# A hybrid SSD and S5 layer: the input projection in two blocks of tokens, each weight tile used twice

## The chip, the cores and the metric

One core of a Trainium2 chip. The metric is the device time in microseconds of one execution. The engines are TensorE (PE, with its weight loads PEld), VectorE (DVE), ScalarE (ACT), GpSimd (POOL) and SyncE (SP), whose queue issues most transfers.

## The reference, cut to what matters

One layer over 1024 prompt tokens and 32 sample tokens, which share the weights:

```
xn = rmsnorm(x, pre_mix_norm_w)
proj = xn @ w_in
z, xbc, dt_raw, u_s5 = split(proj)          # 512, 1024, 8 and 512 columns
y_ssd = ssd_mixer(z, xbc, dt_raw, ...)      # conv of 4 taps + SiLU on xbc, chunked scan, * silu(z), rmsnorm
y_s5  = s5_mixer(u_s5, ...)                 # complex diagonal recurrence, gelu, per-group GLU
h = x + rmsnorm(concat([y_ssd, y_s5]) @ w_out, post_mix_norm_w)
up = causal_dwconv(rmsnorm(h, pre_ffn_norm_w) @ w_up)       # 3 taps
y = h + rmsnorm((gelu(gate) * val) @ w_down, post_ffn_norm_w)
```

## The kernel before

Everything is feature-major: features on partitions, the 1056 tokens along the free axis. Tokens are cut into three chunks of 512, 272 and 272 (`CHUNKS`, L22); chunk 0 is block 0, chunks 1 and 2 are block 1. All products are exact to fp32: weights and activations are split into a high and a low part in fp32r, and `mm3` (L439) makes three products (high by high, high by low, low by high) for each 128 rows of the contraction. With eight such pieces a tile of 128 outputs and one chunk takes 24 products.

**Weights.** `w_load` (L415) brings one tile of 128x1024 from memory (`raw`, two buffers, a transfer of 512 KB on SP), `w_split` (L423) makes the high part on ScalarE (`wh`, a copy by the helper at L253) and the low part on DVE (`wl = raw - wh`, L431); both have two buffers. The sequence of tiles is a list, `order` (L409): sixteen input tiles, then the second half of the output projection's rows for block 0 (`outh`, from S5), its first half (`outs[0]`, from SSD), the same for block 1, and the tiles of the feed-forward network.

**Input projection.** Tiles 0 to 3 give `u` (for S5), 4 to 11 `xBC` (for SSD), 12 to 15 `z` (its gate). Each tile is loaded and split once and used for the three chunks in turn (`gemm_in`, L569); only the last two z tiles are taken as 14 for chunk 0, 15 for chunk 0, then both for the rest (`gemm_z`, L585), so that block 0's z ("zA") is there early. An accumulator (`pm`, from a ring in PSUM) is freed by its evacuation: `evac_xbc` (L483) takes one DVE step (L489) for chunk 0, and then the convolution of block 0 (three DVE steps at L495 on `xo`, with a scaled copy and a SiLU on ScalarE), for the other chunks L500 and L502; `evac_z` (L525) takes two DVE steps (L530, L532) with a tanh on ScalarE in the accumulator between them, and stores z in memory (L533).

**Side work.** Generators are stepped between the products: the S5 preparations and its eight runs (each ends with `y5s`, L923, and a store), `conv_b` (L508; block 1's convolution, eight tiles with three steps at L518 on `xob` and one at L520), `s5mix` (L1238; it reads the results of S5 back in 32 transfers and makes the high and low parts of the mixed features 4 to 7), the SSD scan of block 0 (`frontsA`, `backsA`, `gatesA`), and later, in the feed-forward part, the same of block 1 (`frontsB`, `backsB`, `gatesB`). A generator that yields a name waits for it: `conv_b` begins with `yield par["cvat"]`, which is "run7", the last run of S5. The framework's scheduler then orders the instructions of each engine by data and by priority, so that the order in the program is only a wish.

Of the kernel before, what the change touches and what calls it, by code (L numbers as in the profile page):

```python
# [21 lines left out]
CHUNKS = [(0, WA), (WA, HB), (WA + HB, T - WA - HB)]  # L22
# [25 lines left out]
           cvat='run7', tcat=1, late_at=2, nsq=1, fg=(), fp=((1, 3), (1, 3), (3,)), fch=(0, (0, 1), 2), pfin=0, q0=0, q1=0, q2=0, nb=0,   # L48
# [128 lines left out]
def body(tc, xT, wt, wdt, vec, cst, dtp, hist4, hist3, h0ssd, s5p, s5bc, s5d, glu, glub,  # L177
# [5 lines left out]
    par = dict(PAR)  # L183
# [4 lines left out]
    done = set()  # L188

    def mm(out, lhsT, rhs, start=True, stop=True, **kw):  # L190
        n = rhs.free_size() if hasattr(rhs, "free_size") else int(np.prod(rhs.shape[1:]))
        m = int(np.prod(lhsT.shape[1:]))
        if lhsT.dtype == F32R:
            clk[0] += max(n / 2.36, 107 if m > 64 else 62) * 1e-3
        else:
            clk[0] += max(n * 1.69, 214 if m > 64 else 120) * 1e-3
        PE.matmul(out, lhsT, rhs, start=start, stop=stop, **kw)  # L197
# [34 lines left out]
    def side(name, gen, prio=0, ch=0):  # L232
        sides.append(Side(gen, name, prio, ch))

    def run_main(gen):
        for _ in gen:
            for s in list(sides):
                if s.ready():
                    s.step()
# [12 lines left out]
    def act(out, in_, func, scale=1.0, bias=0.0):  # L252
        S.activation(out, in_, func, bias=bias, scale=scale)  # L253
# [22 lines left out]
    def pmt():  # L276
        pch[1] += 1
        ch = pch[0][pch[1] % len(pch[0])]
        return ms.tile([128, 512], F32, name="pm", tag=f"ms{ch}", bufs=par["msb"][ch])
# [123 lines left out]
    WT = {}  # L403
    ob = par["ob_at"]
    outh = [("out", q) for q in range(4)]
    outs = [[("out", 4 + q, b) for q in range(4)] for b in range(2)]
    ups = [("up", j) for j in range(2 * FF)]
    outh2 = [o + (1,) for o in outh[par["nb"]:]]
    order = [("in", j) for j in range(16)] + outh + outs[0] + outh2 + [u + (0,) for u in ups[:ob]]  # L409
    order += outs[1] + [u + (0,) for u in ups[ob:]] + [u + (1,) for u in ups]  # L410
    seq = [{"in": WIN, "out": WOUT, "up": WUP}[o[0]] + o[1] for o in order]
    pos = {o: i for i, o in enumerate(order)}
# [2 lines left out]
    def w_load(n):  # L415
        while st["load"] <= min(n, len(seq) - 1):
            i = st["load"]
            r = ring.tile([128, 1024], F32, name="raw", tag="raw", bufs=2)
            D.dma_start(r, wt[seq[i]])
            WT[i] = [r]  # L420
            st["load"] += 1

    def w_split(n):  # L423
        while st["split"] <= min(n, len(seq) - 1):
            i = st["split"]
            w_load(i)
            r = WT[i][0]
            hi = ring.tile([128, 1024], F32R, name="wh", tag="wh", bufs=2)
            lo = ring.tile([128, 1024], F32R, name="wl", tag="wl", bufs=2)
            act(hi, r, AF.Copy)  # L430
            V.tensor_tensor(lo, r, hi.bitcast(F32), sub)  # L431
            WT[i] = [hi, lo]
            st["split"] += 1

    def xsl(x, c):
        o = CHUNKS[c][0] - BLK[c > 0][0]
        return [t[:, :, o:o + CHUNKS[c][1]] for t in x[c > 0]]

    def mm3(ps, w, x, ks, first, last):  # L439
        for k in ks:  # L440
            wh, wl = w[0][:, k * 128:k * 128 + 128], w[1][:, k * 128:k * 128 + 128]
            xh, xl = x[0][:, k, :], x[1][:, k, :]
            mm(ps, wh, xh, start=(k == first), stop=False)
            mm(ps, wh, xl, start=False, stop=False)
            mm(ps, wl, xh, start=False, stop=(k == last))
# [7 lines left out]
    X = {}  # L453
# [29 lines left out]
    def evac_xbc(j, c, ps):  # L483
        t0, w = CHUNKS[c]
        eb = XB[1][:, j, :]
        if c == 0:
            e = XB[0][:, j, :3 + WA]
            G.memset(e[:, 0:3], 0.0)
            V.tensor_tensor(e[:, 3:], ps[:, :w], rbc[:, t0:t0 + w], mult)  # L489
            G.tensor_copy(eb[:, 0:3], e[:, WA:])  # L490
            G.tensor_copy(eb[:, 3 + TP - WA:6 + TP - WA], hist4_t[:, j, :])
            o = tl("xo", [128, WA], "xo")
            act(o, e[:, 0:WA], AF.Identity, scale=vc("cw", 4 * j), bias=vc("cb", j))
            for i in range(1, 4):
                V.scalar_tensor_tensor(o, e[:, i:i + WA], vc("cw", 4 * j + i), o, mult, add)  # L495
            act(XB[0][:, j, :WA], o, AF.Silu)
            return
        o = 3 + t0 - WA
        wp = min(w, TP - t0)
        V.tensor_tensor(eb[:, o:o + wp], ps[:, :wp], rbc[:, t0:t0 + wp], mult)  # L500
        if w > wp:
            V.tensor_tensor(eb[:, EB - TS:], ps[:, wp:w], rbc[:, TP:], mult)  # L502
            G.tensor_copy(o4[:, j, 0, :], eb[:, TP - WA:TP - WA + 3])
            G.tensor_copy(o4[:, j, 1, :], eb[:, EB - 3:])
            if j == 7:
                D.dma_start(o_conv, o4)

    def conv_b():  # L508
        yield par["cvat"]
        n = EB - 3  # L510
        cwh = con.tile([128, 40], F32, name="cwh")
        V.tensor_scalar(cwh, vc("cw", 0, 40), 0.5, None, mult)
        for j in range(8):
            e = XB[1][:, j, :]
            o, th = tl(("bc", "PQ")[j % 2], [128, n], "xob"), e[:, 0:n]
            act(o, e[:, 0:n], AF.Identity, scale=cwh[:, 4 * j:4 * j + 1], bias=cwh[:, 32 + j:33 + j])
            for i in range(1, 4):
                V.scalar_tensor_tensor(o, e[:, i:i + n], cwh[:, 4 * j + i:4 * j + i + 1], o, mult, add)  # L518
            act(th, o, AF.Tanh)
            V.scalar_tensor_tensor(e[:, 0:n], th, 1.0, o, add, mult)  # L520
            yield par["cvb"]
# [3 lines left out]
    def evac_z(j, c, ps):  # L525
        t0, w = CHUNKS[c]
        zc[0] += 1
        ps = ps[:, :w]
        zt = tl(("xo", "xe")[zc[0] % 2], [128, 512], "zst")[:, :w]
        V.scalar_tensor_tensor(zt, ps, 0.5, rbc[:, t0:t0 + w], mult, mult)  # L530
        act(ps, zt, AF.Tanh)
        V.scalar_tensor_tensor(zt, ps, 1.0, zt, add, mult)  # L532
        D.dma_start(z_dram[:, j, t0:t0 + w], zt)  # L533
# [32 lines left out]
        w_split(2)  # L566
        yield

    def gemm_in(j0, j1, evac):  # L569
        for j in range(j0, j1):  # L570
            w_split(j)
            for c in range(3):
                t0, w = CHUNKS[c]
                ps = pmt()
                mm3(ps[:, :w], WT[j], xsl(X, c), range(4), 0, 7)
                if c == 0:
                    w_load(j + 2)
                yield
                mm3(ps[:, :w], WT[j], xsl(X, c), range(4, 8), 0, 7)
                evac(j, c, ps)  # L580
                if c == 1:
                    w_split(j + 1)
                yield

    def gemm_z():  # L585
        yield from gemm_in(12, 14, lambda j, c, ps: evac_z(j - 12, c, ps))
        w_split(14)
        for j, c in ((14, 0), (15, 0), (14, 1), (14, 2), (15, 1), (15, 2)):
            t0, w = CHUNKS[c]
            ps = pmt()  # L590
            mm3(ps[:, :w], WT[j], xsl(X, c), range(4), 0, 7)
            if c == 0:
                w_load(j + 2)
            yield
            mm3(ps[:, :w], WT[j], xsl(X, c), range(4, 8), 0, 7)
            evac_z(j - 12, c, ps)
            if j == 15 and c == 0:
                done.add("zA")
            if (j, c) == (14, 0):
                w_split(15)  # L600
            if (j, c) == (14, 2):
                w_split(16)
            yield
        done.add("zdone")

    small = {}

# [425 lines left out]
    pch[0] = par["pch0"]  # L1033
    run_main(gemm_in(3, 4, evac_u))
    run_main(dt_gemm())
    run_main(gemm_in(4, 12, lambda j, c, ps: evac_xbc(j - 4, c, ps)))
    done.add("xbc")
    state = {}
    SC, MIX = {}, {}
# [172 lines left out]
    def fronts(b):  # L1212
        if b:
            yield "convb"
        else:
            for n in ("xbc", "dt", "prep7", "run6"):
                yield n
        for c in SSDC[b]:
            n = 1 if b else 2
            if c - n >= SSDC[b][0]:  # L1220
                yield f"back{c - n}"
            yield from ssd_front(c)
            done.add(f"front{c}")
# [168 lines left out]
            act(rbc[:, t0:t0 + w], norm_r(list(accs.values()), w, scrt("U0", ("W1", "W0")[b]), None, f"p{c}"), AF.Copy)  # L1392
        yield 0

    side("convb", conv_b())
    side("s5mix", s5mix(), par["pg"])
    side("frontsA", fronts(0), par["pf"], par["cf"])
    side("backsA", backs(0), par["pb"], par["cb"])
    side("gatesA", gates_a(), par["pgt"], par["cg"])
    run_main(gemm_z())  # L1400
    finish("s5mix")
    pch[0] = par["pch1"]
    run_main(gemm_outh())
# [215 lines left out]
    def fin_block(b):  # L1619
# [7 lines left out]
        for c in BLKC[b]:  # L1627
            yield from fin_mm(c)
            side(f"fin{c}", fin_out(c), par["pfin"], par["fch"][c])

    side("frontsB", fronts(1), 0, par["cf2"])
    side("backsB", backs(1), 0, par["cb2"])
    side("gatesB", gates(1), 0, par["cg2"])
# [28 lines left out]
```

## Time and profile before

| what | us |
|---|---|
| three runs: median (lowest to highest) | 1337.19 (1330.95 to 1337.25) |
| the profiled execution's own time | 1333.72 |
| its span | 1331.9 |
| PE, PEld, DVE busy in it | 1246.3, 1119.5, 1006.5 |
| ACT, POOL busy in it | 576.4, 403.6 |

The input projection lies between some 30 and 345 us of the span, the first block's output projection begins at 345.6 (second half of its rows) and 395 us, and from there to the end stands the feed-forward network, with the second block's SSD scan beside its first part. The times of rows are microseconds from the span's start. The granted clock of TensorE is given as a share of its full 2.4 GHz.

### The profile page before, as it was taken

How to read it: one execution, taken by the hardware profiler on the slowest of the kernel's cores; microseconds unless marked ns; L12 is line 12 of the kernel's file. 1: busy time of each engine (PE TensorE's matmuls, PEld its weight loads, DVE VectorE, ACT ScalarE, POOL GpSimd, SP SyncE). 2: the span in 40 equal slices, each digit the busy share in tenths (PEclk: the TensorE clock that was granted, in tenths of full speed). 3: DMA queues.
4: the chain of work that ended last, by engine and by line, in shares of the span. 5: the costliest groups of instructions: out<-in, count | busy, mean ns of one | idle time of the engine just before them, and what ended most of it. 6: DMA issues, size and time to landing. Idle time of an engine off the chain costs nothing.

```text
span 1331.9 us, 20957 instructions
## 1 busy us (share of the span) xinstructions
PE 1246.3 (94%) x7880; PEld 1119.5 (84%) x7880; DVE 1006.5 (76%) x1781; ACT 576.4 (43%) x984; POOL 403.6 (30%) x577
## 2 busy tenths in 40 slices
PE   7799889999869899999999999999899999999994
PEld 6678889888748787877897878889899999999994
DVE  8857886996764878887759986677767777777777
ACT  7335655554433545544335433335343333333343
POOL 5453545433424723421035310001511001101013
PEclk9898999999879899999999989999899999999997
DMA  7051333225214532234333333222332222222211
GB/s 229 34 154 41 98 93 98 86 77 141 76 46 135 170 119 88 72 103 129 122 122 113 96 134 95 95 95 80 111 96 95 80 96 82 93 86 87 78 56 68
DMA packets 66902, 132.15 MB, mean 99 GB/s; under 512 B 13936, under 2 KB 34800, under 8 KB 66800
## 3 DMA queue, kind: packets, MB, share of 16 engines
q1 hardware_dynamic: 66800, 130.81, 31.1%
q8 instruction: 62, 1.02, 0.3%
q14 instruction: 40, 0.33, 0.1%
HBM read 111.69 MB, written 15.81 MB: 96 GB/s over the span
## 4 chain that ended last, share of the span: by engine, by line
PE 72%; DVE 15%; ACT 3%; issue 2%; DMA 1%; POOL 1%; SPq 1%; DVEq 0%; ACTq 0%; POOLq 0%
PE pm L197 65%; PE ms L197 7%; DVE wl L431 2%; DVE o L1377 2%; DVE ftmp L1456 1%; DVE acc L1609 1%; DVE xob L518 1%; DVE xo L495 1%; DVE xl L1380 1%; ACT xh L253 1%; DMA raw<-wt 1%; DVE yr L822 1%; DMA y<-yd 0%; PE ms L201 0%; DVE fext L1439 0%
## 5 line engine op out<-in xcount | busy, mean ns | idle before, releaser
L197 PE MATMUL pm<-xh,wh 128*128 128x272 f32 (+1 forms) x1616 | 536.4, 333 | 19.8 <-ACT xh L253 8.7
L197 PE MATMUL pm<-xh,wl 128*128 128x272 f32 (+1 forms) x1616 | 534.5, 332 | 11.6 <-DVE wl L431 11.6
L197 PE MATMUL pm<-xl,wh 128*128 128x272 f32 (+1 forms) x1616 | 533.9, 330 | 0.7 <-DVE xl L763 0.7
L197 PEld LDWEIGHTS pm<-xh,wh 128*128 128x128 f32 x1616 | 312.6, 194 | 44.9 <-ACT xh L253 9.5
L197 PEld LDWEIGHTS pm<-xh,wl 128*128 128x128 f32 x1616 | 311.9, 193 | 34.3 <-DVE wl L431 12.7
L197 PEld LDWEIGHTS pm<-xl,wh 128*128 128x128 f32 x1616 | 312.3, 193 | 23.8 <-DVE xl L763 1.6
L253 ACT ACTIVATE wh<-raw 128x1024 fp32r<-128x1024 f32 x120 | 126.6, 1055 | 175.7 <-PE pm L197 125.7
L431 DVE TENSOR_TENSOR wl<-raw,wh 128x1024 fp32r<-128x1024 f32 x120 | 157.1, 1310 | 43.1 <-ACT wh L253 42.7
L197 PE MATMUL pm<-ah,dh 128*128 128x272 f32 (+1 forms) x528 | 173.1, 328 | 2.1 <-DVE fext L1439 1.3
L197 PE MATMUL pm<-ah,dl 128*128 128x272 f32 (+1 forms) x528 | 172.3, 326 | 0.0
L197 PE MATMUL pm<-al,dh 128*128 128x272 f32 (+1 forms) x528 | 172.1, 326 | 0.0
L1511 DVE TENSOR_TENSOR acc<-acc,pm 128x272 f32<-128x272 f32 (+1 forms) x235 | 121.0, 520 | 55.4 <-PE pm L197 55.0
L1456 DVE SCALAR_TENSOR_TENSOR ftmp<-fext,vec_t,ftmp 128x512 f32<-128x512 f32 (+1 forms) x176 | 138.4, 788 | 1.7 <-ACT ftmp L253 1.0
L1439 DVE TENSOR_TENSOR fext<-pm,rbc 128x512 f32<-128x512 f32 (+2 forms) x132 | 67.2, 510 | 74.3 <-PE pm L197 70.9
L1434 POOL COPY fext<-halo 128x2 f32<-128x2 f32 x88 | 38.0, 432 | 263.6 <-DVE ftmp L1456 245.5
L253 ACT ACTIVATE dh<-raw 128x1024 fp32r<-128x1024 f32 (+1 forms) x46 | 46.8, 1022 | 162.6 <-PE pm L197 135.4
L197 PEld LDWEIGHTS pm<-ah,dh 128*128 128x128 f32 x528 | 99.8, 189 | 11.1 <-DVE fext L1439 2.0
L197 PEld LDWEIGHTS pm<-ah,dl 128*128 128x128 f32 x528 | 99.7, 189 | 8.2
L197 PEld LDWEIGHTS pm<-al,dh 128*128 128x128 f32 x528 | 99.8, 189 | 7.5
L253 ACT ACTIVATE ftmp<-fext,vec_t 128x512 f32<-128x512 f32 (+1 forms) x88 | 72.1, 821 | 20.4 <-DVE fext L1441 13.2
L1489 DVE TENSOR_TENSOR dl<-raw,dh 128x1024 fp32r<-128x1024 f32 (+1 forms) x46 | 54.6, 1188 | 25.1 <-ACT dh L253 24.7
L1451 POOL COPY o<-fext 128x2 f32<-128x2 f32 x44 | 13.8, 313 | 174.8 <-DVE fext L1439 174.8
(318 smaller groups left out, 1693.3 us busy)
## 6 DMA issues: line engine op xcount, KB each, us to landing
raw<-wt SPq DMA_DIRECT2D x164, 512.0 KB, 3.3
gluw<-glu SPq DMA_DIRECT2D x8, 512.0 KB, 4.1
xst<-xT SPq DMA_DIRECT2D x16, 136.0 KB, 4.3
pbd<-pbo SPq DMA_DIRECT2D x8, 272.0 KB, 3.8
xr<-xT SPq DMA_DIRECT2D x8, 272.0 KB, 3.0
pbi<-pbd SPq DMA_DIRECT2D x8, 272.0 KB, 2.8
yT<-acc SPq DMA_DIRECT2D x8, 272.0 KB, 2.2
ud<-uext SPq DMA_DIRECT2D x4, 528.0 KB, 2.9
```

Source lines behind the costliest of these rows:

```text
L197: PE.matmul(out, lhsT, rhs, start=start, stop=stop, **kw)
L253: S.activation(out, in_, func, bias=bias, scale=scale)
L431: V.tensor_tensor(lo, r, hi.bitcast(F32), sub)
L495: V.scalar_tensor_tensor(o, e[:, i:i + WA], vc("cw", 4 * j + i), o, mult, add)
L518: V.scalar_tensor_tensor(o, e[:, i:i + n], cwh[:, 4 * j + i:4 * j + i + 1], o, mult, add)
L1377: V.scalar_tensor_tensor(h, h, vc("post_mix", k), r1, mult, mult)
L1434: G.tensor_copy(e[:, 0:2], halo[:, j, :])
L1439: V.tensor_tensor(e[:, 2 + o:2 + o + wp], ps[:, :wp], rbc[:, t0:t0 + wp], mult)
L1451: G.tensor_copy(o3[:, j, 0, :], e[:, TP - WA:TP - WA + 2])
L1456: V.scalar_tensor_tensor(t, e[:, i:i + n], vc("fw", 3 * j + i), t, mult, add)
L1489: V.tensor_tensor(l, rr, h.bitcast(F32), sub)
L1511: V.tensor_tensor(a, a, ps[:, :w], add)
```

## The change

The list of tiles gets twelve entries more: tiles 4 to 15 are in it twice. `u` is computed for all tokens as before; then tiles 4 to 15 for chunk 0 alone, then 4 to 15 for chunks 1 and 2, with each weight tile fetched and split again (offset 12 in the sequence). `gemm_z` goes. `conv_b` loses its wait for "run7" and is registered just before `frontsB`, at the start of the feed-forward network's side work, instead of ahead of `s5mix`. Line numbers behind the change are 18 lower from L606 on.

```diff
--- before.py
+++ after.py
@@ -406,7 +406,7 @@
     outs = [[("out", 4 + q, b) for q in range(4)] for b in range(2)]
     ups = [("up", j) for j in range(2 * FF)]
     outh2 = [o + (1,) for o in outh[par["nb"]:]]
-    order = [("in", j) for j in range(16)] + outh + outs[0] + outh2 + [u + (0,) for u in ups[:ob]]
+    order = [("in", j) for j in range(16)] + [("in", j, 1) for j in range(4, 16)] + outh + outs[0] + outh2 + [u + (0,) for u in ups[:ob]]
     order += outs[1] + [u + (0,) for u in ups[ob:]] + [u + (1,) for u in ups]
     seq = [{"in": WIN, "out": WOUT, "up": WUP}[o[0]] + o[1] for o in order]
     pos = {o: i for i, o in enumerate(order)}
@@ -506,7 +506,6 @@
                 D.dma_start(o_conv, o4)
 
     def conv_b():
-        yield par["cvat"]
         n = EB - 3
         cwh = con.tile([128, 40], F32, name="cwh")
         V.tensor_scalar(cwh, vc("cw", 0, 40), 0.5, None, mult)
@@ -566,42 +565,25 @@
         w_split(2)
         yield
 
-    def gemm_in(j0, j1, evac):
+    def gemm_in(j0, j1, evac, chunks=range(3), off=0):
         for j in range(j0, j1):
-            w_split(j)
-            for c in range(3):
+            i = j + off
+            w_split(i)
+            for c in chunks:
                 t0, w = CHUNKS[c]
                 ps = pmt()
-                mm3(ps[:, :w], WT[j], xsl(X, c), range(4), 0, 7)
-                if c == 0:
-                    w_load(j + 2)
+                mm3(ps[:, :w], WT[i], xsl(X, c), range(4), 0, 7)
+                if c == chunks[0]:
+                    w_load(i + 2)
                 yield
-                mm3(ps[:, :w], WT[j], xsl(X, c), range(4, 8), 0, 7)
+                mm3(ps[:, :w], WT[i], xsl(X, c), range(4, 8), 0, 7)
                 evac(j, c, ps)
-                if c == 1:
-                    w_split(j + 1)
+                if c == chunks[len(chunks) // 2]:
+                    w_split(i + 1)
                 yield
 
-    def gemm_z():
-        yield from gemm_in(12, 14, lambda j, c, ps: evac_z(j - 12, c, ps))
-        w_split(14)
-        for j, c in ((14, 0), (15, 0), (14, 1), (14, 2), (15, 1), (15, 2)):
-            t0, w = CHUNKS[c]
-            ps = pmt()
-            mm3(ps[:, :w], WT[j], xsl(X, c), range(4), 0, 7)
-            if c == 0:
-                w_load(j + 2)
-            yield
-            mm3(ps[:, :w], WT[j], xsl(X, c), range(4, 8), 0, 7)
-            evac_z(j - 12, c, ps)
-            if j == 15 and c == 0:
-                done.add("zA")
-            if (j, c) == (14, 0):
-                w_split(15)
-            if (j, c) == (14, 2):
-                w_split(16)
-            yield
-        done.add("zdone")
+    def evac_xz(j, c, ps):
+        (evac_xbc if j < 12 else evac_z)(j - 4 if j < 12 else j - 12, c, ps)
 
     small = {}
 
@@ -1033,7 +1015,7 @@
     pch[0] = par["pch0"]
     run_main(gemm_in(3, 4, evac_u))
     run_main(dt_gemm())
-    run_main(gemm_in(4, 12, lambda j, c, ps: evac_xbc(j - 4, c, ps)))
+    run_main(gemm_in(4, 12, evac_xz, (0,)))
     done.add("xbc")
     state = {}
     SC, MIX = {}, {}
@@ -1392,12 +1374,14 @@
             act(rbc[:, t0:t0 + w], norm_r(list(accs.values()), w, scrt("U0", ("W1", "W0")[b]), None, f"p{c}"), AF.Copy)
         yield 0
 
-    side("convb", conv_b())
     side("s5mix", s5mix(), par["pg"])
     side("frontsA", fronts(0), par["pf"], par["cf"])
     side("backsA", backs(0), par["pb"], par["cb"])
     side("gatesA", gates_a(), par["pgt"], par["cg"])
-    run_main(gemm_z())
+    run_main(gemm_in(12, 16, evac_xz, (0,)))
+    done.add("zA")
+    run_main(gemm_in(4, 16, evac_xz, (1, 2), 12))
+    done.add("zdone")
     finish("s5mix")
     pch[0] = par["pch1"]
     run_main(gemm_outh())
@@ -1628,6 +1612,7 @@
             yield from fin_mm(c)
             side(f"fin{c}", fin_out(c), par["pfin"], par["fch"][c])
 
+    side("convb", conv_b())
     side("frontsB", fronts(1), 0, par["cf2"])
     side("backsB", backs(1), 0, par["cb2"])
     side("gatesB", gates(1), 0, par["cg2"])
```

The scheduler decides where things land. Three places on VectorE show it.

First, the projection where SSD's `xBC` tiles are evacuated. `xb_87` is block 0, `xb_88` block 1; `sp`, `dt` belong to the step sizes, `rr`, `R`, `hq`, `yr`, `TC`, `ge`, `y5s` to S5. Before:

```order
L489 TENSOR_TENSOR xb_87<-pm,rbc 128x512
L883 TENSOR_TENSOR hq<-R_1271,TC 128x4x132
L1013 MEMSET dta 32x8
L1014 MEMSET dta 64x8
L819 TENSOR_SCALAR TC<-yr 128x528
L1017 CAST dtah<-dta 128x72
L820 TENSOR_TENSOR yr<-yr,TC 128x528
L1018 TENSOR_TENSOR dtal<-dta,dtah 128x72
L495 SCALAR_TENSOR_TENSOR xo<-xb_87,vec_t,xo 128x512
L822 SCALAR_TENSOR_TENSOR yr<-cst_t,sml,yr 128x132 x4
L923 SCALAR_TENSOR_TENSOR y5s<-ge,y5s 128x528
L500 TENSOR_TENSOR xb_88<-pm,rbc 128x272
```

Now:

```order
L489 TENSOR_TENSOR xb_87<-pm,rbc 128x512
L431 TENSOR_TENSOR wl<-raw,wh 128x1024
L988 TENSOR_SCALAR sp<-sp 128x72
L495 SCALAR_TENSOR_TENSOR xo<-xb_87,vec_t,xo 128x512
L987 TENSOR_TENSOR sp<-sp 128x72
L495 SCALAR_TENSOR_TENSOR xo<-xb_87,vec_t,xo 128x512
L988 TENSOR_SCALAR sp<-sp 128x72
L495 SCALAR_TENSOR_TENSOR xo<-xb_87,vec_t,xo 128x512
L987 TENSOR_TENSOR sp<-sp 128x72
L857 TENSOR_TENSOR rr<-ms_1169,TS 128x264
```

Every 512-wide tile now brings its evacuation, a weight split and three convolution steps in a row; before, the evacuations of the 272-wide chunks and S5 steps lay between.

Second, the end of the projection: the z evacuations (`zst`) and S5's last result. Before (`L1256` makes the low parts of the mixed features, `xl_3448` block 0):

```order
L530 SCALAR_TENSOR_TENSOR zst<-pm,rbc 128x272
L923 SCALAR_TENSOR_TENSOR y5s<-ge,y5s 128x528
L532 SCALAR_TENSOR_TENSOR zst<-pm,zst 128x272
L530 SCALAR_TENSOR_TENSOR zst<-pm,rbc 128x272
L1256 TENSOR_TENSOR xl_3448<-y_3165,xh_3447 128x512
L431 TENSOR_TENSOR wl<-raw,wh 128x1024
```

Now (`L1238` is the line of the low parts, `xl_3673` block 1; `L1126` and `L1165` are SSD's third chunk):

```order
L531 SCALAR_TENSOR_TENSOR zst<-pm,zst 128x272
L1126 TENSOR_TENSOR y_3087<-y_3087,ms_3153 128x512
L1165 TENSOR_TENSOR y_3087<-y_3087,z_3163 128x512
L529 SCALAR_TENSOR_TENSOR zst<-pm,rbc 128x272
L431 TENSOR_TENSOR wl<-raw,wh 128x1024
L1238 TENSOR_TENSOR xl_3673<-y_3131,xh_3672 128x544
L531 SCALAR_TENSOR_TENSOR zst<-pm,zst 128x272
L905 SCALAR_TENSOR_TENSOR y5s<-ge,y5s 128x528
```

The result of S5's run 7 lies behind the last z evacuation; before, four z evacuations followed it.

Third, the second block's output projection in the feed-forward part (`o`, L1340 before and L1322 now, is its evacuation; `gscr` the gate's norm of the 32 sample tokens, `xl_3659` and `xl_3673` its mixed features). Before:

```order
L365 SCALAR_TENSOR_TENSOR gscr<-cst_t,nry,gscr 32x32 x2
L1439 TENSOR_TENSOR fext<-pm,rbc 128x512
L1489 TENSOR_TENSOR dl<-raw,dh 128x1024
L431 TENSOR_TENSOR wl<-raw,wh 128x1024
L1456 SCALAR_TENSOR_TENSOR ftmp<-fext,vec_t,ftmp 128x512 x2
L1466 TENSOR_TENSOR ftmp<-ftmp 128x512
L1439 TENSOR_TENSOR fext<-pm,rbc 128x512
L1166 TENSOR_TENSOR y_5895<-y_5895,ms_6149 128x4x32
L431 TENSOR_TENSOR wl<-raw,wh 128x1024
...
L1170 SCALAR_TENSOR_TENSOR xl_3659<-y_5895,vec_t,xh_3658 128x32 x4
```

Now:

```order
L1322 TENSOR_TENSOR o_6302<-pm,pbi 128x272
L338 TENSOR_TENSOR nra<-nry 128x2
L339 SCALAR_TENSOR_TENSOR nra<-nra,nrt 128x2
L340 SCALAR_TENSOR_TENSOR nry<-nra,nry 128x2
...
L364 TENSOR_SCALAR gscr<-cst_t,nry 32x32 x2
L365 SCALAR_TENSOR_TENSOR gscr<-cst_t,nry,gscr 32x32 x2
L1148 TENSOR_TENSOR y_6211<-y_6211,ms_6286 128x4x32
L1152 SCALAR_TENSOR_TENSOR xl_3673<-y_6211,vec_t,xh_3672 128x32 x4
L1322 TENSOR_TENSOR o_6302<-pm,pbi 128x272 x2
```

Two evacuations of the output projection now stand ahead of the gate's norm; before, the mixed features were done ahead of the first of them.

## Rows read from the trace of the kernel before

**Rows 1.** The page, part 1: busy time, share of the span, instructions.

```profile
PE 1246.3 (94%) x7880; PEld 1119.5 (84%) x7880; DVE 1006.5 (76%) x1781; ACT 576.4 (43%) x984; POOL 403.6 (30%) x577
```

**Rows 2.** Stretches: PE, PEld, DVE, ACT, POOL busy (instructions); granted clock, DMA share, GB/s.

```profile
110.00:200.00 90.00, 82.26 (x557) 76.62 (x557) 72.58 (x134) 57.51 (x124) 43.05 (x48) 0.96 0.30 86
200.00:246.00 46.00, 46.00 (x320) 42.62 (x319) 32.92 (x57) 23.70 (x58) 24.70 (x25) 1.00 0.31 90
246.00:291.00 45.00, 40.78 (x277) 38.21 (x277) 42.87 (x68) 25.76 (x56) 13.90 (x11) 0.96 0.27 80
...
320.00:345.50 25.50, 17.96 (x131) 15.98 (x129) 17.11 (x20) 13.54 (x18) 11.08 (x7) 0.83 0.49 124
...
378.00:397.00 19.00, 7.52 (x35) 4.52 (x34) 15.93 (x51) 5.53 (x17) 6.32 (x6) 0.68 0.08 28
600.00:640.00 40.00, 40.00 (x196) 31.10 (x196) 28.96 (x54) 14.69 (x22) 4.48 (x11) 1.00 0.39 128
```

**Rows 3.** Weight tiles, 95 to 350 us: count, min/median/max ns, first and last start.

```profile
L253 ACT ACTIVATE wh<-raw x12: 1040/1050/1069, 124.6 to 335.5; 128x1024 fp32r<-128x1024 f32 x12
L431 DVE TENSOR_TENSOR wl<-raw,wh x12: 1207/1224/2017, 125.6 to 337.0; 128x1024 fp32r<-128x1024 f32 x12
L419 SPq DMA_DIRECT2D raw<-wt x12: 327/358/415, 130.1 to 338.3; - x12
```

**Rows 4.** Timeline of PE: start, duration; neighbours of a 512-wide and a 272-wide tile.

```profile
296.21 0.39 PE L197 MATMUL pm<-xh,wh 128*128 128x512 f32 x1
296.44 0.39 PE L197 MATMUL pm<-xl,wh 128*128 128x512 f32 x1
...
311.80 0.30 PE L197 MATMUL pm<-xh,wl 128*128 128x272 f32 x1
311.93 0.29 PE L197 MATMUL pm<-xh,wh 128*128 128x272 f32 x1
```

**Rows 5.** Waits of SP's queue, 95 to 350 us: total, times, longest.

```profile
SPq L419 <- DVE wl L431: 23.6, 6, 7.9
```

**Rows 6.** Groups of VectorE, 110 to 200 us: busy, mean ns of one, idle before.

```profile
L495 DVE SCALAR_TENSOR_TENSOR xo<-xb,vec_t,xo 128x512 f32<-128x512 f32 x13 | 12.6, 966 | 4.6 <-ACT xo L253 4.5
L431 DVE TENSOR_TENSOR wl<-raw,wh 128x1024 fp32r<-128x1024 f32 x4 | 6.5, 1618 | 0.3 <-ACT wh L253 0.3
```

**Rows 7.** Timeline of PE, waits in brackets, around the end of the projection.

```profile
328.66 0.40 PE L197 MATMUL pm<-xh,wh 128*128 128x272 f32 x1 [2.75 <-DVE zst L532]
...
341.95 1.98 PE L197 MATMUL ms<-cst_t,dta 128*64 128x128 f32 x16 [4.07 <-ACT E L253]
343.71 1.92 PE L197 MATMUL ms<-E,xdt 128*64 128x128 f32 x16
...
383.93 0.61 PE L197 MATMUL ms<-onec,z 128*128 128x1 f32 x4 [3.54 <-POOL z L1185]
```

**Rows 8.** Timelines of VectorE and SP: run 7 of S5 and its way back.

```profile
317.25 2.05 DVE L923 SCALAR_TENSOR_TENSOR y5s<-ge,y5s 128x528 f32<-128x528 f32 x1
326.04 1.08 DVE L1256 TENSOR_TENSOR xl<-y,xh 128x512 fp32r<-128x512 f32 x1 [4.49 <-ACT xh L253]
335.32 1.10 DVE L1256 TENSOR_TENSOR xl<-y,xh 128x512 fp32r<-128x512 f32 x1 [0.59 <-ACT xh L253]
...
329.16 1.89 SPq L1246 DMA_DIRECT2D y<-yd x4
```

**Rows 9.** Timelines of VectorE and PE: the gate of the 32 sample tokens.

```profile
641.15 0.14 DVE L321 TENSOR_SCALAR nrt<-ms 32x2 f32<-32x2 f32 x1
645.84 0.40 DVE L365 SCALAR_TENSOR_TENSOR gscr<-cst_t,nry,gscr 32x32 fp32r<-32x32 f32 x2
656.71 0.73 DVE L1170 SCALAR_TENSOR_TENSOR xl<-y,vec_t,xh 128x32 fp32r<-128x32 f32 x4
...
653.16 0.41 PE L197 MATMUL ms<-gscr,ones_r 32*128 32x64 f32 x2
```

**Rows 10.** Groups of VectorE, 95 to 397 us: the convolution of block 1.

```profile
L518 DVE SCALAR_TENSOR_TENSOR xob<-xb,cwh,xob 128x547 f32<-128x547 f32 x24 | 21.8, 932 | 0.1
```

## The prediction, made before the changed kernel was run

> **What bounds the kernel now.** I began with the page's first part: TensorE (PE) is busy for 94% of the span, VectorE (DVE) for 76% [rows 1]. The change does not alter one matrix product, so only idle time of PE can come or go. Next I cut the time around the input projection into stretches [rows 2]. The stretch 200 to 246 us is a pure PE stretch (46.00 of 46.00). In 110 to 200 us PE idles 7.7 us with DVE at 72.6 of 90; in 246 to 291 us, where the convolution of the rest stands, DVE is busy 42.87 of 45 and PE loses 4.2 us; from 320 to 345.5 us PE loses 7.5 us, from 378 to 397 us 11.5 us. In the up-projection (600 to 640 us) PE has no idle time at all and DVE 28% of it. So a gain can only come from some 31 us of idle time ahead of 397 us, and a loss from whatever fills DVE in the projection or holds PE where it now never waits.
>
> **The sum** is made against the profiled execution, 1333.7 us; it lies 3.5 us under the median of the three runs, 1337.19 us. About half a per cent (6.7 us) is what a measurement of this kernel can tell from no change, so "same" is 1330.5 to 1343.9 us.
>
> *Twelve more weight splits, in the projection.* Each of tiles 4 to 15 is fetched and split twice: 12 more copies on ScalarE, 12 more subtractions on DVE, 12 more transfers issued by SP. A copy takes 1.05 us on an engine at 57.5 of 90 us, an issue on SP 0.36 us [rows 2, 3]; I take both at nothing, under cover of PE, which needs 24 x 0.227 = 5.4 us for one tile of 512 tokens [rows 4] (without that cover a late tile costs 0.36 + 1.05 + 1.2 = 2.6 us and its flight; SP does stand behind late splits for 23.6 us already, 7.9 us at most [rows 5]). The DVE subtraction is the dear one: median 1.224 us, between 1.207 and 2.017 us [rows 3], and 1.618 us on average in 110 to 200 us [rows 6], where GpSimd (POOL) is busy 43 of 90 us [rows 2].
>
> The order makes it worse for the first 512 tokens. All eight convolutions of that block (three steps each, 24) and twelve splits now stand in one block of 512-wide tiles; in 110 to 200 us there were 13 such steps and 4 splits [rows 6]. PE would pass about nine tiles in that time at the same pace. DVE then gets (24 - 13) x 0.966 = 10.6 us of convolution and 5 x 1.618 = 8.1 us of splits more, 18.7 us on the 17.4 us that it has free: it is full. The S5 recurrence, whose steps share DVE and feed PE, is pushed back. From 110 to 291 us DVE has 148.4 us of 181 now and would have some 164, so on average it isn't the bound; hence the ends: nothing (S5 slides into the freer stretches behind) and 18.7 us (all of it is waited for). The nearest row is 246 to 291 us, DVE at 95% and PE losing 4.2 of 45 us, 9.4%. The same loss on the 90 us of a full DVE is 8.4 us: **+8**.
>
> By the Trainium skill, "GPSIMD Engine Reference", section "1. Specifications", GpSimd shares its SBUF interfaces with VectorE and contends with VectorE instructions that have two SBUF inputs. The trace agrees as far as it goes (1.618 us on average where GpSimd is busy half the time, 1.207 us at best); by that rule all twelve could cost 24.2 us of DVE in place of 19.4, 5 us more in the crowded block.
>
> *The z tiles of the last two chunks, eight 272-wide in a row.* Before, 512-wide ones lay between. Each accumulator stays taken through two DVE steps and a tanh, and PE passes a tile in 24 x 0.127 = 3.0 us [rows 4]. Such a wait shows at 328.66 us, 2.75 us [rows 7]. Ends 0 and three of them, 8 us; I take **+2**.
>
> *The first block's tail.* Since all inputs of the first 512 tokens come early, its SSD scan is about one chunk further when the projection ends. Three waits then lose their cause: 2.75 us at 328.66, 4.07 us at 341.95, 3.54 us at 383.93 us [rows 7], together -10.4 us. Against it: run 7 of S5 now stands last. Before, its result was formed at 317.25 us, written out, read back by 16 small transfers on SP (the last four issued at 329.16 us, behind a weight load and a z store), and its last low part was done at 336.4 us, 19.2 us later, all of it under projection tiles; without SP's delay (first low part done at 327.1 us) it is about 10 us [rows 8]. In the new order that result lies behind every z evacuation. The chain of 10 to 19 us, 15 in the middle, has SSD products (1.98 + 1.92 us in the row behind 341.95 and alike) and the first half of two output tiles beside it, which I put at 10 us. So 5 us show: -10.4 + 5, **-5** (ends -10.4 and +8.8).
>
> *The SSD scan of the rest, in the up-projection.* The order shows its last chunk (the 32 sample tokens) slide past the first two tiles of the second output projection. Before, the gate's norm began on DVE at 641.15 us, its scale was spread by PE at 653.16 us and its last low part was done at 657.44 us [rows 9], before the output needed it. Its own path is 641.15 to 646.24 us, then 653.16 to 657.44 us: 5.1 + 4.3 = 9.4 us. In the new order one group of 24 narrow products (3.0 us) stands between the sums and the spread, and about as much behind it; 9.4 - 6 leaves 3.4 us for PE to wait in a stretch where it never waited. **+4**, ends 0 and 9.4.
>
> *The convolution of the rest.* The diff drops its wait for run 7 and registers it far later. The order leaves its 24 steps of 0.932 us [rows 10] in the projection, among runs 6 and 7 and the z evacuations; no part of it stands in the up-projection. Cost **0**. Were it there, 22 us on a DVE with 11 free of each 40 would still fit.
>
> 8 + 2 - 5 + 4 = +9: 1333.7 + 9 = **1343 us**.
>
> **Rivals.**
> - *The projection stays a PE stretch* (faster). The new splits fall into DVE's gaps, run 7's chain is covered, and PE gets its three waits back: 1333.7 - 10.4 = 1323 us. For it: PE at 46.00 of 46.00 with DVE at 32.9, and 15 us of DVE free between 200 and 291 us. Against it: it needs DVE to stay under some 80% in the block that I count full. It decides if the evacuations of the first block do not delay PE.
> - *DVE bounds the first block* (slower). All 18.7 us are waited for, z costs 2, and run 7, pushed later still, takes the tail's gain back: 1333.7 + 18.7 + 2 + 0 + 4 = 1358 us. It decides from the point at which S5 steps that PE waits for queue behind convolutions. For it: 18.7 us do not fit into 17.4. Against it: S5 had 26 us of slack (317 against 345 us).
> - *Nothing that counts*: the convolution is not later in fact, the extra work is hidden, tail and gate cancel (-5 + 4): 1333 us.
>
> **How the numbers follow.** The forecast 0.45 (its own range 1335 to 1351 us: slower 0.23, same 0.20, faster 0.02); PE-bound projection 0.20, all faster; DVE-bound block 0.22, all slower; nothing 0.13 (same 0.09, faster 0.04). Faster 0.26, same 0.29, slower 0.45. The range runs from the one rival to the other: 1323 to 1358 us.
>
> **What would show it.** In the changed profile: 12 more rows of the subtraction with a mean over 1.3 us; a stretch of some 70 to 90 us behind 110 us with DVE over 90% and PE under that; the y5 loads behind the projection's end and a wait of PE for the copies of run 7; no 3.5 us wait ahead of the first gate; a wait of PE of some us where the second output projection begins. Wrong if PE is full in the first block, or if a wait that I have not named exceeds 8 us.

## The result, and the profile after

The changed kernel took 1342.26 us (median of 10 runs, 1339.51 to 1346.61) against 1331.76 us before (10 runs): a ratio of 1.0073, 95% interval 1.0052 to 1.0094. That is slower, by 0.7%, and 0.7 us from the forecast of 1343 us. The four terms behind that forecast did not fare as well.

The profiled execution of the change took 1345.64 us, span 1343.9. Its busy time, beside [rows 1]:

```profile
PE 1253.2 (93%) x7880; PEld 1118.7 (83%) x7880; DVE 1025.5 (76%) x1793; ACT 585.1 (44%) x994; POOL 409.9 (31%) x577
```

VectorE has 12 instructions and 19 us more. TensorE has as many products as before and 7 us more of busy time: some products took longer, which idle time does not show.

The stretches that answer to [rows 2], same columns, and one more, 665 to 675 us:

```profile
110.00:200.00 90.00, 83.07 (x443) 70.32 (x443) 80.77 (x131) 58.97 (x121) 42.22 (x38) 0.95 0.36 106
200.00:246.00 46.00, 45.28 (x354) 43.95 (x354) 36.48 (x61) 26.06 (x66) 23.48 (x27) 1.00 0.49 140
246.00:291.00 45.00, 40.22 (x311) 39.20 (x311) 44.83 (x70) 25.41 (x53) 22.37 (x19) 0.96 0.29 91
320.00:345.50 25.50, 24.25 (x202) 21.82 (x202) 20.29 (x27) 12.59 (x28) 9.32 (x6) 1.00 0.38 110
378.00:397.00 19.00, 12.34 (x51) 8.67 (x49) 14.02 (x43) 9.08 (x21) 3.60 (x4) 0.87 0.25 83
600.00:640.00 40.00, 40.00 (x204) 31.50 (x203) 32.37 (x53) 17.86 (x25) 10.02 (x16) 1.00 0.33 106
665.00:675.00 10.00, 6.68 (x38) 6.11 (x39) 5.34 (x24) 2.09 (x7) 1.88 (x4) 0.83 0.22 77
```

From 110 to 200 us VectorE went from 72.6 to 80.8 us, not to 90, and PE lost no more than before (6.9 us against 7.7). The hole at 320 to 345.5 us is closed (24.25 us busy against 17.96). The new hole is the last row: in ten microseconds PE is busy for 6.68, at a granted clock of 0.83.

Weight tiles in 95 to 350 us ([rows 3]), VectorE's groups in 110 to 200 us ([rows 6]), and SP's wait ([rows 5]):

```profile
L253 ACT ACTIVATE wh<-raw x24: 1042/1054/1062, 101.6 to 338.5; 128x1024 fp32r<-128x1024 f32 x24
L431 DVE TENSOR_TENSOR wl<-raw,wh x24: 1199/1223/2812, 103.8 to 339.6; 128x1024 fp32r<-128x1024 f32 x24
```

```profile
L495 DVE SCALAR_TENSOR_TENSOR xo<-xb,vec_t,xo 128x512 f32<-128x512 f32 x22 | 22.7, 1032 | 0.2
L431 DVE TENSOR_TENSOR wl<-raw,wh 128x1024 fp32r<-128x1024 f32 x9 | 12.2, 1352 | 0.8 <-ACT wh L253 0.7
```

```profile
SPq L419 <- DVE wl L431: 48.0, 12, 11.7
```

The block of 512-token tiles is there: 22 convolution steps and 9 splits in the stretch that held 13 and 4. SP stood behind splits twice as long (48.0 us against 23.6), but no weight copy waited for a load there.

Where the time went is read from two evacuations that both kernels have: of the first output projection (`pao`, first and last of 8) and of the second (`pbi`, first and last of 16). Before, then the change:

```profile
L1340 DVE TENSOR_TENSOR o<-pm,pao x8: 678/691/692, 403.1 to 418.7; 128x512 f32<-128x512 f32 x8
L1340 DVE TENSOR_TENSOR o<-pm,pbi x16: 434/442/443, 661.4 to 683.4; 128x272 f32<-128x272 f32 x16
```

```profile
L1322 DVE TENSOR_TENSOR o<-pm,pao x8: 678/691/692, 405.8 to 421.4; 128x512 f32<-128x512 f32 x8
L1322 DVE TENSOR_TENSOR o<-pm,pbi x16: 431/434/442, 667.2 to 694.4; 128x272 f32<-128x272 f32 x16
```

Up to the first output projection the change is 2.7 us late, at the end of the second 11.0 us. So 8.3 of 11 us come between the two, and at the second: its 16 evacuations take 27.2 us where they took 22.0, and its 192 products start within 33.2 us (659.80 to 693.03) where they started within 23.9 us (659.10 to 683.03). The timeline of PE there, waits in brackets:

```profile
666.97 0.29 PE L197 MATMUL ms<-onec,z 128*32 128x1 f32 x4 [2.01 <-POOL z L1139]
667.72 0.40 PE L197 MATMUL pm<-xh,wh 128*128 128x272 f32 x1 [0.46 <-DVE nrt L321]
...
668.92 0.43 PE L197 MATMUL pm<-xl,wh 128*128 128x272 f32 x1
669.15 0.43 PE L197 MATMUL pm<-xh,wl 128*128 128x272 f32 x1
...
672.44 0.41 PE L197 MATMUL ms<-gscr,ones_r 32*128 32x64 f32 x2
673.65 0.52 PE L197 MATMUL pm<-xh,wh 128*128 128x272 f32 x2 [0.81 <-ACT xh L253]
```

The gate of the 32 sample tokens is late, as forecast: PE waits for its squares (2.01 us) and its mixed features (0.81 us). Behind the first wait the 272-wide products start every 0.23 us, not every 0.13 us as in [rows 4]: the clock fell to 1.2 GHz for some 3 us.

The 0.46 us between them is put down to the gate's norm, which was the last to end on VectorE. But a `pm` product needs a free accumulator, and the gate's sums lie in another buffer (L272, L279). As the code hands accumulators out, the third tile that PE comes to here takes the accumulator of the first one. The first evacuation, which frees it, ends at 667.66 us: it had waited for its addend `pbi`, the part of the sum that S5's rows gave, read back from memory. The first reload before, and then reload and evacuation in the change:

```profile
630.03 0.33 SPq L1327 DMA_DIRECT2D pbi<-pbd  x1
```

```profile
663.05 0.80 SPq L1309 DMA_DIRECT2D pbi<-pbd  x2
...
667.22 0.44 DVE L1322 TENSOR_TENSOR o<-pm,pbi 128x272 f32<-128x272 f32 x1 [1.05 <-DMA pbi<-pbd]
```

So a second thing is late beside the gate: the first two reloads are issued 4 us ahead of the first evacuation, not 31 us. With the squares in time, the third tile would, by this trace, have waited for the same accumulator until 667.7 us.

### The profile page after: what moved, and what is told of

Its sections match the earlier page's. It is cut to its first block, busy times and chain, and to the rows that moved or that the text cites. A ratio compares the mean times of both kernels' runs of the same rounds, so it can differ in the third digit from the quotient of the medians.

```text
span 1343.9 us, 21034 instructions
## 1 busy us (share of the span) xinstructions
PE 1253.2 (93%) x7880; PEld 1118.7 (83%) x7880; DVE 1025.5 (76%) x1793; ACT 585.1 (44%) x994; POOL 409.9 (31%) x577
## 4 chain that ended last, share of the span: by engine, by line
PE 69%; DVE 15%; DMA 4%; issue 3%; ACT 2%; POOL 2%; SPq 1%; DVEq 0%; ACTq 0%; POOLq 0%
PE pm L197 63%; PE ms L197 6%; DVE wl L431 2%; DMA raw<-wt 1%; POOL pacc L1366 1%; DVE xob L517 1%; POOL o L1360 1%; DMA pbi<-pbd 1%; DVE xo L495 1%; ACT wh L253 1%; DVE o L1359 1%; DVE acc L1593 1%; DVE R L862 1%; DVE xl L1238 1%; DVE yr L804 1%
## 5 line engine op out<-in xcount | busy, mean ns | idle before, releaser
L253 ACT ACTIVATE wh<-raw 128x1024 fp32r<-128x1024 f32 x132 | 139.3, 1056 | 200.4 <-PE pm L197 138.9
L431 DVE TENSOR_TENSOR wl<-raw,wh 128x1024 fp32r<-128x1024 f32 x132 | 170.7, 1294 | 59.2 <-ACT wh L253 58.9
L253 ACT ACTIVATE ftmp<-ftmp 128x512 f32<-128x512 f32 (+1 forms) x44 | 28.4, 646 | 80.7 <-DVE ftmp L1440 80.6
```

## The experiments

Two theories. **A**: what costs is the place of block 1's SSD scan in the program. It may only start when the convolution is finished (`fronts(1)` begins with `yield "convb"`), and that now takes eight steps of the feed-forward part, so the sample tokens' gate comes late. **B**: what costs is the twelve splits on a crowded VectorE. Four kernels were compared with before first (e4's second pass doubles the projected values of the last two chunks, since the high part stands for the low one).

**e1**, the convolution registered where it was:

```diff
     def conv_b():
+        yield par["cvat"]
...
+    side("convb", conv_b())
     side("s5mix", s5mix(), par["pg"])
...
-    side("convb", conv_b())
     side("frontsB", fronts(1), 0, par["cf2"])
```

> The change, but the convolution of the rest is registered ahead of s5mix again, with its wait for run 7, as before. Theory A (what costs is that the scan of the rest waits in program order for a convolution that is registered with it, so the sample tokens' gate comes late at the second output projection): about 8.5 us come back, 1334 us, the gate's norm of the sample tokens stands ahead of the first evacuation again, and PE has no wait there. Theory B (what costs is the twelve extra splits on a crowded VectorE in the projection): nothing comes back, 1342 us.

Measured 1336.29 us (12 runs), ratio 1.0025 (1.0008 to 1.0042).

**e2**, the kernel before with the late registration alone: the last lines of e1's diff the other way round, and no `yield par["cvat"]`.

> The kernel before, with only the late registration of the convolution (no wait for run 7, just ahead of the scan of the rest); projection and weights untouched. Theory A: some 8.5 us slower than before, about 1340 us, by waits of PE and a lower granted clock where the second output projection begins. Theory B: as before, 1332 us.

Measured 1342.73 us (6 runs), ratio 1.008 (1.0056 to 1.0105).

**e3**, the kernel before with twelve double splits:

```diff
             V.tensor_tensor(lo, r, hi.bitcast(F32), sub)
+            if 4 <= i < 16:
+                act(hi, r, AF.Copy)
+                V.tensor_tensor(lo, r, hi.bitcast(F32), sub)
             WT[i] = [hi, lo]
```

> The kernel before, where each of the tiles 4 to 15 is split a second time into the same buffers from the same load: 12 more copies on ScalarE and 12 more subtractions on VectorE, no more transfers. Theory A: they lie beside PE's products, 0 to 3 us slower, at most 1335 us. Theory B: they are waited for, some 8 us slower, 1340 us or more (12 x 1.31 = 15.7 us if all are).

Measured 1339.67 us (9 runs), ratio 1.0057 (1.0037 to 1.0077).

**e4**, the change without the second low parts (for an entry of the list with three members, `lo = hi`):

> The change without the twelve subtractions of the second pass: for the tiles 4 to 15 of the last two chunks the product with the low part of the weights uses the high part in its place, so the output lacks that correction; loads, copies and all products stay. Theory A: 0 to 3 us faster than the change, 1339 to 1342 us, the waits at the second output projection stay. Theory B: 8 us or more faster, 1334 us or less.

Measured 1336.13 us (12 runs), ratio 1.0015 (0.9997 to 1.0033).

Both theories had a part of it. Registration alone makes the old kernel 0.8% slower, and undoing it takes back 0.5% of the change; twelve splits alone make the old kernel 0.6% slower, and without their VectorE half the change loses 0.6%. Stages tell them apart (the last table of this section): e2 loses 9 us from the first output projection to the end of the second, like the change (8), e1 and e3 lose 1 to 2. What e3 loses lies ahead of the first output projection: from block 0's last `xBC` evacuation to there it takes 165.1 us, against 156.9 in before, 157.2 in e2 and 156.9 in e8, so 8.2 us more. (At the first output projection itself only 4.9 us of them show against before, whose profile had lost some 3 us more to the low clock of the last section.) At e2's second output projection stand the same waits as in the change:

```profile
661.13 0.29 PE L197 MATMUL ms<-onec,z 128*32 128x1 f32 x4 [2.01 <-POOL z L1156]
662.65 0.59 PE L197 MATMUL pm<-xh,wh 128*128 128x272 f32 x1 [1.24 <-DVE nrt L321]
...
667.33 0.41 PE L197 MATMUL ms<-gscr,ones_r 32*128 32x64 f32 x2
668.54 0.52 PE L197 MATMUL pm<-xh,wh 128*128 128x272 f32 x2 [0.80 <-ACT xh L253]
```

The second of them, 1.24 us, again lasts until the first evacuation is done (662.59 us), and that had waited 1.82 us for `pbi`.

Then three more. **e5** keeps the late registration and writes the convolution in one step; **e6** and **e7** are e1 with all, or every other one, of the second-pass subtractions on GpSimd.

```diff
             V.scalar_tensor_tensor(e[:, 0:n], th, 1.0, o, add, mult)
-            yield par["cvb"]
+        yield par["cvb"]
```

```diff
-            V.tensor_tensor(lo, r, hi.bitcast(F32), sub)
+            (G if order[i][0] == "in" and len(order[i]) == 3 else V).tensor_tensor(lo, r, hi.bitcast(F32), sub)
```

(In e7 the condition also asks for `i % 2`.)

> The change, with the convolution of the rest still registered just ahead of the scan of the rest, but written out in one step (it yields once at its end, not after each of its eight tiles), so the scan behind it starts some eight steps earlier in the program. Theory A (the scan's place in the program, which waits for the convolution's eight steps, is what costs): as with the early registration, about 1336 us, the gate ahead of the first evacuation and no wait of PE at the second output projection. Rival C (late registration costs through the convolution itself, which lands in another place or at another priority): 1342 us as the change, since the convolution is as late and as low as before.

Measured 1326.43 us (12 runs), ratio 0.9953 (0.9932 to 0.9975): faster than both kernels, and 10 us better than theory A expected. The late registration is harmless; its eight steps were not. Of the 10 us, 7.4 are in the tail (column b below, against e1).

> The change with the early registration of e1, and the twelve subtractions of the second pass on GpSimd in place of VectorE; nothing is left out. In the trace of the change a two-input GpSimd operation of 128x1024 takes 2.23 us, so 27 us more on an engine that was busy 131 of 290 us. If the twelve VectorE subtractions are what the new order pays (theory B for the first half): the first output projection starts some 6 to 10 us earlier than in e1, 1326 to 1330 us, faster than both kernels. If GpSimd's part lies on the path of S5 (it makes half of hq, for which PE waited 6 us), or if VectorE operations next to it grow as much as it saves: 1334 to 1340 us.

Measured 1352.81 us (6 runs), ratio 1.0146 (1.0118 to 1.0174).

> As e6, but only six of the twelve subtractions of the second pass, those of every other tile, on GpSimd. If the gain is by the work taken from VectorE: between e1 and e6, about 1332 us. If GpSimd becomes the late engine in e6, this one is the fastest of the three, at most 1332 us.

Measured 1341.33 us (6 runs), ratio 1.0072 (1.0047 to 1.0098). Both missed: taking work from VectorE made the rest of the projection longer, by 10.6 us for six subtractions and 16.0 us for twelve (column a below, against e1). Groups of VectorE in 195 to 345 us, in e1, which differs in the subtractions alone, and then in e6 (busy, mean ns of one, idle before):

```profile
L518 DVE SCALAR_TENSOR_TENSOR xob<-xb,cwh,xob 128x547 f32<-128x547 f32 x24 | 24.7, 1043 | 0.0
L520 DVE SCALAR_TENSOR_TENSOR xb<-xb,xob 128x547 f32<-128x547 f32 x8 | 6.2, 795 | 0.0
```

```profile
L518 DVE SCALAR_TENSOR_TENSOR xob<-xb,cwh,xob 128x547 f32<-128x547 f32 x24 | 29.9, 1270 | 0.0
L520 DVE SCALAR_TENSOR_TENSOR xb<-xb,xob 128x547 f32<-128x547 f32 x8 | 8.1, 1020 | 0.0
```

And the subtraction itself on GpSimd in e6, in 195 to 360 us:

```profile
L431 POOL TENSOR_TENSOR wl<-raw,wh x12: 2356/2442/3098, 202.5 to 340.7; 128x1024 fp32r<-128x1024 f32 x12
```

The same convolution step takes 1.270 us beside a busier GpSimd (95.3 of 150 us, against 76.3 in e1) and 1.043 us without; e7 lies between (1.138 us at 82.0). This is the rule cited in the prediction (the Trainium skill, "GPSIMD Engine Reference", "1. Specifications": GpSimd and VectorE share SBUF interfaces, and VectorE instructions with two SBUF inputs contend). The trace agrees with it, at 22% on such a step. VectorE was left with 123 us of work in that stretch in place of 127, though 13 of its 14 splits there were gone. The 32 convolution steps grew by 7.1 us in all; where the rest of the 16 us comes from is not shown. The granted clock of the stretch is also lower (0.93 against 0.98). PE's wait for GpSimd's part of `hq`, the other reason that the expectation named, did not grow (6.9 us against 6.7).

Last, two that part what e5 is made of. **e8** is the kernel before with e5's convolution alone; **e9** is e5 without the second low parts, by e4's edit.

> The kernel before with e5's way of the convolution alone (registered late, without a wait for run 7, in one step), the input projection untouched. If e5's gain is the new order of the projection's: 1330 to 1335 us, as before. If it is the late one-step convolution's: 1326 to 1328 us, as e5, and the order of the blocks is worth nothing.

Measured 1332.61 us (12 runs), ratio 1.0002 (0.9986 to 1.0018): the convolution's form is worth nothing by itself on the kernel before. With e2 it shows the eight steps a second time: the same late registration costs 0.8% in eight steps and nothing in one. And e5's half per cent needs both, the new order and the one step: the new order with the early convolution (e1) measured 1.0025.

> e5 without the twelve subtractions of the second pass (the product with the low part uses the high part there, so the projected values of the last two chunks are doubled); loads, copies and products stay. Price of the subtractions where nothing else disturbs: theory A 0 to 3 us, 1323 to 1326 us; theory B some 8 us, 1318 us.

Measured 1327.04 us (12 runs), ratio 0.9952 (0.9936 to 0.9968): the same as e5. By stages it is not nothing, though. All stages, in us, worked out from the first and last starts of VectorE's evacuations in each profile (a: last `xBC` evacuation of block 0 to last z evacuation, given where the order is the new one; b: from there to the first output projection's first evacuation; c: from there to the last of the second output projection):

| kernel | a | b | c | ratio to before |
|---|---|---|---|---|
| before | | 55.2 | 280.3 | 1 |
| the change | 160.4 | 64.0 | 288.6 | 1.0073 |
| e1, early convolution | 160.1 | 64.1 | 281.2 | 1.0025 |
| e2, before + late convolution | | 57.2 | 289.6 | 1.0080 |
| e3, before + 12 splits | | 58.6 | 282.6 | 1.0057 |
| e4, change - 12 subtractions | 155.3 | 62.7 | 288.8 | 1.0015 |
| e5, late convolution in one step | 162.0 | 56.7 | 280.9 | 0.9953 |
| e6, e1 with 12 on GpSimd | 176.1 | 66.1 | 282.4 | 1.0146 |
| e7, e1 with 6 on GpSimd | 170.7 | 61.5 | 282.3 | 1.0072 |
| e8, before + one step | | 55.3 | 282.0 | 1.0002 |
| e9, e5 - 12 subtractions | 156.6 | 61.2 | 281.3 | 0.9952 |

Column c has two values: 288.6 to 289.6 us where the convolution is late in eight steps, 280.3 to 282.6 us elsewhere. The first reload of `pbi` parts the kernels in the same way: it is issued 4 to 5 us ahead of the first evacuation that needs it in the change, e2 and e4, and 31 to 35 us ahead in all others. So the eight steps are the cause of the 8 us; how much of it goes by the gate and how much by the reload no run parts. Column a gives the price of the twelve subtractions twice: 160.4 - 155.3 = 5.1 us in the change, 162.0 - 156.6 = 5.4 us in e5. In the new order column b is 61.2 to 66.1 us where run 7 of S5 ends behind the last z evacuation. In the change (VectorE's timeline):

```profile
341.77 0.45 DVE L531 SCALAR_TENSOR_TENSOR zst<-pm,zst 128x272 f32<-128x272 f32 x1
342.12 2.24 DVE L905 SCALAR_TENSOR_TENSOR y5s<-ge,y5s 128x528 f32<-128x528 f32 x1
```

and in e5, the only kernel of the new order where it ends before:

```profile
331.04 0.71 DVE L905 SCALAR_TENSOR_TENSOR y5s<-ge,y5s 128x528 f32<-128x528 f32 x1 [0.20 <-ACT y5s L253]
...
337.57 0.44 DVE L531 SCALAR_TENSOR_TENSOR zst<-pm,zst 128x272 f32<-128x272 f32 x1
```

Run 7 alone does not make the difference of 7.3 us, though. PE's waits for the copies behind it are 5.56 us in the change and still 4.26 us in e5 (1.32 + 2.12 + 0.82). The whole stretch b in the change, then in e5, columns as in [rows 2]:

```profile
341.77:405.80 64.03, 49.54 (x248) 37.42 (x248) 42.44 (x77) 25.20 (x45) 18.55 (x13) 0.87 0.31 81
```

```profile
337.57:394.26 56.69, 44.60 (x238) 33.89 (x238) 38.66 (x76) 24.14 (x43) 18.54 (x13) 0.94 0.26 73
```

PE is idle for 14.5 us against 12.1 and busy for 49.5 us against 44.6, at a granted clock of 0.87 against 0.94. Two thirds of the difference are thus busy time, and what lowered the clock was not tested.

In e9 the result is formed at 333.9 us, again behind the last z evacuation (333.5 us): it gains 5.4 us in a and gives back 4.5 in b, which leaves its time at e5's. That the scheduler moved run 7 there is seen, why it did is not; no run forces its place alone.

## Why the prediction was right, and where its steps were not

The sign and the size were right, and PE does wait for the sample tokens' gate at the second output projection. The split of the sum was not right, and that the total came so near is in part luck: by the profiles it was 2.3 us too high up to the first output projection and 4.3 us too low behind it.

- **Twelve splits, +8.** Right in kind and too high for the new order: 5.1 and 5.4 us (a, and the copies on ScalarE are not in it), a third of their 16 us. In the old order, copies included, the like cost 8.2 us (e3). VectorE wasn't full in 110 to 200 us (80.8 of 90), since S5 slid, the lower end named in the prediction. The step that failed is the scaling by VectorE's share: in 110 to 200 us VectorE rose by 8.2 us and PE's loss went from 7.7 to 6.9 us, and in the row that I scaled, 246 to 291 us, PE loses 4.8 us with VectorE at 44.8 of 45 us.
- **z tiles back to back, +2.** Too dear: waits of PE for z evacuations sum to 1.1 us in the change, against 3.1 us before.
- **The first block's tail, -5.** This term failed, and not by run 7. PE's idle time from 291 us to the first output projection is 19.1 us in the change (114.80 - 95.73) and was 19.7 us before (112.10 - 92.45):

```profile
291.00:405.80 114.80, 95.73 (x612) 80.39 (x611) 82.52 (x129) 48.78 (x90) 42.64 (x32) 0.91 0.34 94
```

```profile
291.00:403.10 112.10, 92.45 (x561) 77.03 (x560) 73.83 (x118) 44.73 (x82) 40.61 (x30) 0.89 0.30 86
```

  The failed step is "three waits then lose their cause". The 3.54 us for the gate are gone and of the 2.75 us for z 1.13 are left, but the 4.07 us for `E` came back as 3.44 us, 38 us earlier:

```profile
303.67 1.98 PE L197 MATMUL ms<-cst_t,dta 128*64 128x128 f32 x16 [3.44 <-ACT E L253]
```

  Two waits came that the prediction did not name, 2.03 us for `xdt` and 1.4 us more for the gated `y`, while the waits for `scr` fell by 2.6 us. "5 us show" of run 7's way back was right, at 1.07 + 2.87 + 1.62 = 5.56 us around the first output tiles:

```profile
353.03 0.73 PE L197 MATMUL pm<-xh,wh 128*128 128x512 f32 x2 [1.07 <-ACT xh L253]
...
359.48 0.73 PE L197 MATMUL pm<-xh,wh 128*128 128x512 f32 x2 [2.87 <-ACT xh L253]
...
366.47 0.50 PE L197 MATMUL pm<-xl,wh 128*128 128x512 f32 x1 [1.62 <-DVE xl L1238]
```

  Against [rows 8], run 7's result came 24.9 us later (342.12 against 317.25 us) while the projection ended 6 us earlier (last z step at 341.8 against 347.9 us). Work only moved behind that end, so the terms ahead of it and behind it can't be read one by one. Together they were put at +8 +2 -5 = +5, and +2.7 us were measured at the first output projection. In e5 it is a gain of some 4 us: 394.3 against 403.1 us, less some 5 us of low clock that the profile of before has and e5's lacks (last section).
- **The sample tokens' gate, +4.** Mis-sized by half: it cost 8.3 us (c), near the end of 9.4 that the prediction kept. The waits for the gate make 2.01 + 0.81 us; the rest is products that take longer and the wait for an accumulator (0.46 us). Two parts that the prediction left out are seen, the clock (products at 0.23 in place of 0.13 us for some 3 us, about 1.4 us) and 28 small products of the scan between the wide ones, which take 3.5 us there and were done elsewhere before. The late reload is a third, whose share is not known.
- **The convolution of the rest, 0.** Right for its own 24 steps, which stayed in the projection, and blind to what waits for it: its eight steps, registered late, are the cause of the term above (the change against e5, e2 against e8). The order showed the slide, and I priced it without asking why.

The faster rival's time is near what the change could have been: the new order without the eight steps took 1326.4 us (e5) against 1323. It gets there another way, since in e5 the subtractions still cost 5.4 us and PE still waits 4.3 us for the copies of run 7.

## What to carry to other kernels

When a step moves later in a program that a scheduler reorders, price what waits for its name, not the step itself: here 31.5 us of convolution stayed in the projection and the scan that asks for it moved, for 8 us. A change of two parts should be measured as two: the new order with the convolution in one step was worth half a per cent, and the eight steps made a loss of 0.7% of it. Moving two-input work from VectorE to GpSimd was no relief here, where both were busy. And a wait that the profile puts down to one instruction should be checked against what the product needs: here it was an accumulator, held by a late reload.

## What the runs showed that was not expected

The clock can fall with no idle time ahead of it. From 105 to 115 us, where 512-wide products alternate with products of 16x8, PE was busy for all 10 us in the change and in e5 alike, and for the 15 us ahead of them, with a granted clock of 0.51 in the one and 1.00 in the other:

```profile
105.00:115.00 10.00, 10.00 (x29) 7.26 (x29) 6.64 (x15) 2.31 (x4) 2.00 (x3) 0.51 0.16 52
```

```profile
105.00:115.00 10.00, 10.00 (x63) 8.52 (x63) 8.76 (x19) 5.69 (x9) 2.41 (x6) 1.00 0.19 58
```

The order of PE's products is the same there; why the clock fell in one and not in the other is open. The profiles of before, e6 and e7 have the drop too (0.50, 0.53, 0.53), those of e1, e4 and e9 do not, and e2, e3 and e8 have a shorter one (0.83). It makes some 5 us: block 0's first to last `xBC` evacuation takes 79.5 us in the change, e6 and e7, and 74.7 to 75.2 us in e1, e4, e5 and e9. So single profiles of this kernel are to be compared by stages, and small ratios by many runs.
